# A two-layer trunk on one core: TensorE's order in the RWKV stage pinned by rounds, and the chunk's triangular system solved in two halves of 64 tokens

## The chip, the core and the metric

The kernel runs on one core of one Trainium2 chip. The time is device microseconds from start to end of one execution; lower is better. Beside the timed runs there is one profiled execution, whose trace gives the start and length of every instruction on every engine. TensorE (PE in the trace) does matmuls and transposes, each with a weight load (PEld); VectorE is DVE, ScalarE is ACT, GpSimd is POOL, and SyncE (SP) issues the loads.

## The reference, cut to what matters

One sequence of 256 tokens with 2048 channels passes an RWKV-7 layer and then an attention layer, each followed by a squared-ReLU MLP. The change touches only the RWKV-7 mixer, whose core is a recurrence over tokens for 32 heads of 64 channels:

```python
rkv = jnp.einsum('jbtd,jde->jbte', xs[:3], w_rkv)
...
def step(S, inp):
    r_t, w_t, k_t, v_t, kk_t, a_t = inp
    sa = jnp.einsum('bhvk,bhk->bhv', S, -kk_t)
    S = (S * w_t[:, :, None, :]
         + sa[..., None] * (kk_t * a_t)[:, :, None, :]
         + v_t[..., None] * k_t[:, :, None, :])
    y_t = jnp.einsum('bhvk,bhk->bhv', S, r_t)
    return S, y_t
```

The kernel does it in two chunks of 128 tokens. Within a chunk the step becomes a unit lower triangular system of 128 unknowns for each head; its inverse, transposed, is what the kernel calls `Tt`. The chunks are joined by the state `S`.

## The kernel before

Weights come in as float32 and are used as a sum of two reduced-precision parts: `hilo` makes `whi` on ACT (L162) and `wlo` on DVE (L163), and a product is three matmuls (`mm3w`, L213 to L215: hi times hi, hi times lo, lo times hi). A weight unit of 128x2048 is cast in two halves of 1024 columns. Each half also calls `pump`, which deals out the later layers' conditioning vectors: one step is a load and a DVE multiply with a sum over 128x1024 (L310).

The RWKV stage has 16 tiles of 128 channels (two heads each). For tile i two things are made:

- `project_rk(i)`, the products for r and k: 2 weights by 16 channel blocks by 3 matmuls of 256 columns, all into the PSUM bank `rk`. It gives way after every second channel block, 16 times in all.
- `rwkv_tile(i)`, the recurrence, a generator of 27 pieces with a `yield` between them. In order: 1 loads of small weights; 2 decay and gate (`wa`, the scan `cum`); 3 to 5 norms and scaled r, k (`st`, `AR`, `bt`, `kt`); 6 the masked matrices `MB` (`pm<-AR,bt`, then ACT copies and a POOL mask); 7 transposes (`tr`, `bk`); 8 the 16x16 diagonal blocks `Dg` spread out into `Z` on DVE; 9 the matmul `ar<-Z` (L710) and the matrices `MK` (`pm<-AR,kt`); 10 to 12 fifteen steps of forward substitution on DVE, two small instructions each (`xt<-ar,X` L722 and `X<-X,xt` L723), then ACT copies into `T16` and a DVE transpose `Tn` (L748); 13, 14 join blocks of 16 to 32 (`pW` L753, `pN` L762); 15, 16 join 32 to 64 (L777, L785); 17 to 19 join 64 to 128 (transpose `pT` L793, `pW` L799, `pN` L805, with ACT copies into `T64`, `W64` and `Tt`); then for chunk 0 `U = Tt * rhs` (`pu` L825), the state (`psS`) and the output (`py`), for chunk 1 the right side (`prhs<-S`), `pu` and `py`; then a group norm (`mean`, `var`, an inverse root of ten tiny DVE instructions) and the gated output (`yt`).

The driver (L903 on) works in rounds. A tile is started every STAGGER = 9 rounds, up to three fly at once, and in each round every flying tile does one piece, oldest first. So three tiles stand nine pieces apart: piece 9 of one shares its round with piece 18 of the tile before and piece 27 of the one before that. After the pieces, `16 / STAGGER` parts of the next tile's r and k products are recorded.

Recording isn't issuing. A scheduler takes the recorded program, plays its own timing model, and writes a fixed queue for each engine; when two instructions are ready it prefers the one recorded earlier. On the chip each engine then works through its queue strictly in that order. PSUM tiles go round in pools (`rt` and `rb` with 2 banks each, `mm` 2, `rk` 1), and `whi`/`wlo` have 2 buffers each.

When the last tile has started, `out_start` (the output projection's first 12 blocks, `pos`) takes the place of the r and k products.

Of the kernel before, what the change touches and what calls it, by code (L numbers as in the profile page):

```python
# [20 lines left out]
P = 128  # L21
D = 2048
KT = D // P
T = 256
# [9 lines left out]
STAGGER = 9  # L34
XV = 2
RATE_R = 0.85
RATE_T = 0.75
PACE = 2.5
RATE_M = 0.68
RATE_L = 0.25  # L40
RATE_H = 1.0
# [35 lines left out]
def trunk_kernel(ctx: ExitStack, tc: tile.TileContext, a, out, dbg=None):  # L77
# [300 lines left out]
    with ExitStack() as s0:  # L378
# [162 lines left out]
        with ExitStack() as s2:  # L541
# [9 lines left out]
            def tmp(tag, shape=(T,), bufs=1, dt=F32):  # L551
                return p5.tile([P, *shape], dt, tag=tag, name=tag, bufs=bufs)
# [13 lines left out]
            def project_rk(i):  # L566

                ps = banks["rk"].tile([P, 512], F32, tag="rk", name="rk")
                res = []
                for w, name in enumerate(("wr", "wk")):  # L570
                    raw = load(a[name][i])
                    o = slice(w * T, (w + 1) * T)
                    for half in range(2):
                        hi = split["hi"].tile([P, 1024], F32R, tag="whi", name="whi")
                        lo = split["lo"].tile([P, 1024], F32R, tag="wlo", name="wlo")
                        hilo(hi, lo, raw[:, half * 1024 : half * 1024 + 1024])
                        pump(rate[0])
                        for j in range(8):
                            kt = half * 8 + j
                            s = slice(j * P, (j + 1) * P)  # L580
                            mm3w(ps[:, o], hi[:, s], lo[:, s], xs_at(w, 0, kt), xs_at(w, 1, kt), kt == 0, kt == KT - 1)
                            if j % 2:
                                yield
                    res.append(tmp("rk"[w] + "S"))
                    ACT.copy(res[w], ps[:, o])  # L585
                rks[i] = res

            def rwkv_tile(i):
                K1 = DL + 1

                def tbank(name, k):
                    return banks[k].tile([P, 512], F32, tag=k, name=name)
# [80 lines left out]
                def At(m):  # L673
                    return MB[:, m // 2, m % 2, 0, :]
# [113 lines left out]
                yield  # L788

                lo, hi = slice(0, 64), slice(64, 128)  # L790
                pT = tbank("pT", "rt")
                for m_ in range(4):
                    PE.transpose(pT[lo, m_ * 64 : m_ * 64 + 64], Tt[lo, m_, lo], ident[lo, lo])  # L793
                T64 = tmp("T64", (4, 64))
                ACT.copy(T64[lo], pT[lo, :T].rearrange("p (m t) -> p m t", m=4))
                yield
                pW = tbank("pW", "rt")
                for m_ in range(4):
                    PE.matmul(pW[hi, m_ * 64 : m_ * 64 + 64], At(m_)[lo, hi], T64[lo, m_, :], start=True, stop=True)  # L799
                W64 = T64  # L800
                ACT.copy(W64[hi], pW[hi, :T].rearrange("p (m t) -> p m t", m=4))
                yield
                pN = tbank("pN", "rt")
                for m_ in range(4):
                    PE.matmul(pN[lo, m_ * 64 : m_ * 64 + 64], W64[hi, m_, :], Tt[hi, m_, hi], start=True, stop=True)  # L805
                ACT.copy(Tt[lo, :, hi], pN[lo, :T].rearrange("p (m t) -> p m t", m=4))
                yield

                S = tmp("S", (P,), 2)
                POOL.memset(S, 0.0)  # L810
                py = banks["py"].tile([P, 512], F32, tag="py", name="py")
                for c in range(2):
                    if c:
                        pr = tbank("prhs", "rb")
                        PE.matmul(pr[:, :P], AR[:, c, 0, :], S, start=True, stop=False)
                        for h in range(2):
                            vs = V[:, c, i * P + h * 64 : i * P + h * 64 + 64]
                            PE.matmul(pr[:, h * 64 : h * 64 + 64], MK[:, h, c, 0, :], vs, start=False, stop=(h == 1))
                        rh = tmp("rh", (P,), 3)
                        ACT.copy(rh, pr[:, :P])  # L820
                        yield
                    pu = tbank("pu", "rb")
                    for h in range(2):
                        q = slice(h * 64, h * 64 + 64)
                        PE.matmul(pu[:, q], Tt[:, 2 * h + c, :], rh[:, q], start=True, stop=True)  # L825
                    U = tmp("U", (P,), 2)
                    ACT.copy(U, pu[:, :P])
                    yield
                    if c == 0:
                        psS = tbank("psS", "rb")  # L830
                        for h in range(2):
                            q = slice(h * 64, h * 64 + 64)
                            vs = V[:, 0, i * P + h * 64 : i * P + h * 64 + 64]
                            PE.matmul(psS[q, :64], bk[:, q], U[:, q], start=True, stop=False)
                            PE.matmul(psS[q, :64], bk[:, P + h * 64 : P + h * 64 + 64], vs, start=False, stop=True)
                            ACT.activation(S[q, q], psS[q, :64], AF.Copy, scale=sc[q, 1:2])
                    else:
                        PE.matmul(py[:, P:T], AR[:, c, 1, :], S, start=True, stop=False)
                    for h in range(2):
                        q = slice(h * 64, h * 64 + 64)  # L840
                        vs = V[:, c, i * P + h * 64 : i * P + h * 64 + 64]
                        o = py[:, c * P + h * 64 : c * P + h * 64 + 64]
                        PE.matmul(o, MB[:, h, c, 1, :], U[:, q], start=(c == 0), stop=False)
                        PE.matmul(o, MK[:, h, c, 1, :], vs, start=False, stop=(c == 0 or h == 1))
                    if c == 0:
                        yield
# [2 lines left out]
                mean = tmp("mean", (4,))  # L849
                DVE.tensor_reduce(mean, py3, AX.X, ALU.add)  # L850
                DVE.tensor_scalar(mean, mean, 1.0 / 64, None, ALU.mult)
                yield
                tr = tbank("tr", "rb")
                for c in range(2):
                    PE.transpose(tr[:, c * P : (c + 1) * P], V[:, c, i * P : (i + 1) * P], ident)
# [45 lines left out]
            for _ in project_rk(0):  # L901
                pass
            flying, nxt, steps = [], 0, 0  # L903
            fill, owed, pace = iter(()), 0.0, 16 / STAGGER
            while nxt < KT or flying:
                if nxt < KT and len(flying) < LONG and steps >= STAGGER * nxt:
                    for _ in fill:
                        pass
                    flying.append(rwkv_tile(nxt))
                    nxt += 1  # L910
                    if nxt < KT:
# [1 line left out]
                    else:  # L913
# [3 lines left out]
                            "p (t k) c -> p t (k c)", t=2)  # L917
                        fill, pace = out_start(), PACE
                        rate[0] = RATE_T
                steps += 1  # L920
                for g_ in list(flying):
                    if next(g_, 0) == 0:
                        flying.remove(g_)

                owed += pace if flying else 48
                while owed >= 1:
                    owed -= 1
                    next(fill, 0)
            for _ in fill:
                pass  # L930
            for i in range(KO, KT):
# [632 lines left out]
```

## Time and profile before

| | |
|---|---|
| Timed runs | 2624.5, 2628.51, 2627.69 us; median 2627.69 |
| Profiled execution | 2610.6 us, span of its instructions 2608.9 us, granted TensorE clock 0.989 |
| Busy over the span | PE 96%, PEld 80%, DVE 75%, ACT 50%, POOL 3% |
| HBM read | 589.89 MB, 227 GB/s over the span |
| RWKV stage | first `rk` product at 211.7 us, last `pos` at 795.7 us |
| In 441.00 to 472.00 us (31 us) | PE busy 29.25, DVE 25.34, ACT 19.22, POOL 3.20 us |

PE's matmuls are pipelined, so their lengths overlap: an `rk` matmul lasts 0.28 us in the trace, but the next one starts 0.12 us later. What counts for a queue is therefore the step from start to start. "Idle before" in brackets is time the engine stood still, with what ended it. The granted clock is given for a stretch; 1.00 is full speed.

### The profile page before, as it was taken

The numbers are of one execution on the slowest core, as the hardware profiler recorded it, in microseconds if no ns is written. First come the engines' busy times: TensorE is split into PE (matmuls) and PEld (weight loads), VectorE is DVE, ScalarE is ACT, GpSimd is POOL, SyncE is SP. The second block draws the span as 40 slices with busy tenths as digits, with TensorE's granted clock in tenths as the row PEclk, the third lists the DMA queues.
The fourth block names the chain that finished last, engine by engine and source line by source line (L and its number), as shares of the span: only waits on it lengthen the run. The fifth ranks groups of instructions, "written<-read, shape, count | busy, mean of one in ns | idle before, by whom it ended". The sixth has DMA issues, their size and how long they took to land.

```text
span 2608.9 us, 39245 instructions
## 1 busy us (share of the span) xinstructions
PE 2510.7 (96%) x15048; PEld 2077.0 (80%) x15048; DVE 1950.6 (75%) x3823; ACT 1314.7 (50%) x2361; POOL 65.9 (3%) x150
## 2 busy tenths in 40 slices
PE   6998999999997999999999999999899999999998
PEld 3667888888776888888888878788788888888886
DVE  4797888888877788888888868777677655565555
ACT  4555666666745444444444446544544444444443
POOL 0000111011100000000000000000000000000000
PEclk9999999999999999999999999999999999999999
DMA  9755444444466588888888834657657555555553
GB/s 374 304 192 202 155 170 157 166 158 171 167 227 258 201 337 316 329 332 325 333 316 331 328 140 139 211 178 263 219 210 260 192 193 187 187 191 194 187 186 127
DMA packets 87885, 594.54 MB, mean 228 GB/s; under 512 B 10128, under 2 KB 14480, under 8 KB 16784
## 3 DMA queue, kind: packets, MB, share of 16 engines
q1 hardware_dynamic: 87696, 592.03, 62.9%
q8 instruction: 118, 1.93, 0.3%
q14 instruction: 71, 0.58, 0.1%
HBM read 589.89 MB, written 2.10 MB: 227 GB/s over the span
## 4 chain that ended last, share of the span: by engine, by line
PE 87%; DVE 7%; ACT 3%; DMA 2%; issue 1%; POOL 0%; SPq 0%; DVEq 0%; ACTq 0%
PE pup L223 17%; PE pd L208 9%; PE pd L210 9%; PE pd L209 9%; PE pup L224 9%; PE rk L213 2%; PE rk L215 2%; PE rk L214 2%; PE pm L658 2%; DVE wlo L163 2%; PE po L209 1%; PE po L210 1%; PE po L208 1%; PE pv L209 1%; PE pv L210 1%
## 5 line engine op out<-in xcount | busy, mean ns | idle before, releaser
L162 ACT CAST whi<-raw 128x1024 fp32r<-128x1024 f32 x729 | 743.7, 1023 | 882.7 <-PE pd L210 356.3
L163 DVE TENSOR_TENSOR wlo<-raw,whi 128x1024 fp32r<-128x1024 f32 x729 | 865.2, 1189 | 430.1 <-ACT whi L162 427.0
L223 PE MATMUL pup<-h,whi 128*128 128x512 f32 x1920 | 677.8, 398 | 0.0
L224 PE MATMUL pup<-h,wlo 128*128 128x256 f32 x1920 | 539.7, 281 | 0.0
L223 PEld LDWEIGHTS pup<-h,whi 128*128 128x128 f32 x1920 | 361.0, 188 | 88.2
L208 PE MATMUL pd<-whi,uh 128*128 128x512 f32 x1024 | 399.2, 390 | 0.0
L210 PE MATMUL pd<-whi,ul 128*128 128x512 f32 x1024 | 398.9, 390 | 0.0
L209 PE MATMUL pd<-wlo,uh 128*128 128x512 f32 x1024 | 398.8, 389 | 0.0
L310 DVE SCALAR_TENSOR_TENSOR raw<-raw,crow 128x1024 f32<-128x1024 f32 x320 | 388.5, 1221 | 10.5 <-DMA raw<-in_adat_dram 10.2
L224 PEld LDWEIGHTS pup<-h,wlo 128*128 128x128 f32 x1920 | 363.4, 189 | 0.5
L210 PEld LDWEIGHTS pd<-whi,ul 128*128 128x128 f32 x1024 | 192.3, 188 | 40.2
L208 PEld LDWEIGHTS pd<-whi,uh 128*128 128x128 f32 x1024 | 192.3, 188 | 39.9
L209 PEld LDWEIGHTS pd<-wlo,uh 128*128 128x128 f32 x1024 | 192.3, 188 | 39.5
L213 PE MATMUL rk<-xs,whi 128*128 128x256 f32 x512 | 155.2, 303 | 2.8 <-ACT rS L585 2.2
L215 PE MATMUL rk<-xs,wlo 128*128 128x256 f32 x512 | 149.6, 292 | 2.0 <-DVE wlo L163 2.0
L214 PE MATMUL rk<-xs,whi 128*128 128x256 f32 x512 | 147.1, 287 | 0.0
L213 PEld LDWEIGHTS rk<-xs,whi 128*128 128x128 f32 x512 | 98.5, 192 | 13.8 <-issue 8.9
L215 PEld LDWEIGHTS rk<-xs,wlo 128*128 128x128 f32 x512 | 98.4, 192 | 4.7 <-DVE wlo L163 2.8
L214 PEld LDWEIGHTS rk<-xs,whi 128*128 128x128 f32 x512 | 98.5, 192 | 0.9
L722 DVE TENSOR_TENSOR xt<-ar,X 128x60 f32<-128x60 f32 (+14 forms) x240 | 49.5, 206 | 17.5 <-ACT ar L711 14.8
L1180 DVE TENSOR_TENSOR ya<-pd,ya 128x512 f32<-128x512 f32 x96 | 61.5, 682 | 0.0
L209 PE MATMUL pv<-wlo,xsv 128*128 128x512 f32 x128 | 52.8, 413 | 5.5 <-DVE wlo L163 5.3
(431 smaller groups left out, 3671.3 us busy)
## 6 DMA issues: line engine op xcount, KB each, us to landing
raw<-in_adat_dram SPq DMA_DIRECT2D x160, 1024.0 KB, 6.9
raw<-in_up_dram SPq DMA_DIRECT2D x128, 1024.0 KB, 4.9
raw<-in_dn_dram SPq DMA_DIRECT2D x128, 1024.0 KB, 4.9
early<-in_ada_dram SPq DMA_DIRECT2D x17, 1024.0 KB, 11.6
raw<-in_wr_dram SPq DMA_DIRECT2D x16, 1024.0 KB, 4.9
raw<-in_wk_dram SPq DMA_DIRECT2D x16, 1024.0 KB, 5.0
raw<-in_wo_dram SPq DMA_DIRECT2D x16, 1024.0 KB, 5.8
raw<-in_mo_dram SPq DMA_DIRECT2D x16, 1024.0 KB, 4.9
```

The source lines that it names most:

```text
L162: ACT.copy(hi, x)
L163: return DVE.tensor_sub(lo, x, hi.bitcast(F32))
L208: PE.matmul(ps, lh, rh, start=start, stop=False)
L209: PE.matmul(ps, lh, rl, start=False, stop=False)
L210: PE.matmul(ps, ll, rh, start=False, stop=stop)
L213: PE.matmul(ps, wh, xh, start=start, stop=False)
L214: PE.matmul(ps, wh, xl, start=False, stop=False)
L215: PE.matmul(ps, wl, xh, start=False, stop=stop)
L223: PE.matmul(ps, hi[:, s], x2[:, kt].rearrange("p e t -> p (e t)"), start=(kt == 0), stop=False)
L224: PE.matmul(ps[:, T:], lo[:, s], x2[:, kt, 0, :], start=False, stop=(kt == KT - 1))
L310: DVE.scalar_tensor_tensor(raw[:, s], raw[:, s], 1.0, crow[:, s], ALU.mult, ALU.mult, accum_out=part[:, kt, half : half + 1])
L1180: DVE.tensor_add(y, pss[t], y)
```

## The change

1. Each round's recording is put into a block in which TensorE's order is kept as recorded (`tc.manual_schedule`), until `out_start` begins. As the built queues show, the order is kept within the block of one round; the first rows of a block can still move ahead of the rest of an earlier block.
2. `project_rk` gives way after every channel block (32 parts), and `LEAN` says how many parts each of the nine rounds gets, in place of an even share.
3. Pieces 17 to 19 are gone. `Tt` stays block diagonal (two blocks of 64). Each chunk is solved by halves instead: `U[lo] = Tt[lo] * rhs[lo]` (`pu`), then `rhs[hi] += A * U[lo]` (`pA` on PE, an addition of 64x128 on DVE, new line L817), then `U[hi] = Tt[hi] * rhs[hi]` (`pu`). That is four more yields, three fewer for the pieces gone, and one taken out after `mean`: a tile still has 27 pieces.
4. In `psS` the two products with `U` stand before the two with `V`, and the scaling copies after both.

```diff
--- before.py
+++ after.py
@@ -36,6 +36,8 @@
 RATE_R = 0.85
 RATE_T = 0.75
 PACE = 2.5
+
+LEAN = (7, 1, 5, 3, 5, 3, 1, 7, 0)
 RATE_M = 0.68
 RATE_L = 0.25
 RATE_H = 1.0
@@ -579,8 +581,7 @@
                             kt = half * 8 + j
                             s = slice(j * P, (j + 1) * P)
                             mm3w(ps[:, o], hi[:, s], lo[:, s], xs_at(w, 0, kt), xs_at(w, 1, kt), kt == 0, kt == KT - 1)
-                            if j % 2:
-                                yield
+                            yield
                     res.append(tmp("rk"[w] + "S"))
                     ACT.copy(res[w], ps[:, o])
                 rks[i] = res
@@ -788,24 +789,6 @@
                 yield
 
                 lo, hi = slice(0, 64), slice(64, 128)
-                pT = tbank("pT", "rt")
-                for m_ in range(4):
-                    PE.transpose(pT[lo, m_ * 64 : m_ * 64 + 64], Tt[lo, m_, lo], ident[lo, lo])
-                T64 = tmp("T64", (4, 64))
-                ACT.copy(T64[lo], pT[lo, :T].rearrange("p (m t) -> p m t", m=4))
-                yield
-                pW = tbank("pW", "rt")
-                for m_ in range(4):
-                    PE.matmul(pW[hi, m_ * 64 : m_ * 64 + 64], At(m_)[lo, hi], T64[lo, m_, :], start=True, stop=True)
-                W64 = T64
-                ACT.copy(W64[hi], pW[hi, :T].rearrange("p (m t) -> p m t", m=4))
-                yield
-                pN = tbank("pN", "rt")
-                for m_ in range(4):
-                    PE.matmul(pN[lo, m_ * 64 : m_ * 64 + 64], W64[hi, m_, :], Tt[hi, m_, hi], start=True, stop=True)
-                ACT.copy(Tt[lo, :, hi], pN[lo, :T].rearrange("p (m t) -> p m t", m=4))
-                yield
-
                 S = tmp("S", (P,), 2)
                 POOL.memset(S, 0.0)
                 py = banks["py"].tile([P, 512], F32, tag="py", name="py")
@@ -819,20 +802,35 @@
                         rh = tmp("rh", (P,), 3)
                         ACT.copy(rh, pr[:, :P])
                         yield
-                    pu = tbank("pu", "rb")
+
+                    pu = tbank("pu", "rt")
                     for h in range(2):
                         q = slice(h * 64, h * 64 + 64)
-                        PE.matmul(pu[:, q], Tt[:, 2 * h + c, :], rh[:, q], start=True, stop=True)
+                        PE.matmul(pu[lo, q], Tt[lo, 2 * h + c, lo], rh[lo, q], start=True, stop=True)
                     U = tmp("U", (P,), 2)
-                    ACT.copy(U, pu[:, :P])
+                    ACT.copy(U[lo], pu[lo, :P])
+                    yield
+                    pu = tbank("pA", "rt")
+                    for h in range(2):
+                        q = slice(h * 64, h * 64 + 64)
+                        PE.matmul(pu[hi, q], At(2 * h + c)[lo, hi], U[lo, q], start=True, stop=True)
+                    DVE.tensor_add(rh[hi], pu[hi, :P], rh[hi])
+                    yield
+                    pu = tbank("pu", "rt")
+                    for h in range(2):
+                        q = slice(h * 64, h * 64 + 64)
+                        PE.matmul(pu[hi, q], Tt[hi, 2 * h + c, hi], rh[hi, q], start=True, stop=True)
+                    ACT.copy(U[hi], pu[hi, :P])
                     yield
                     if c == 0:
                         psS = tbank("psS", "rb")
-                        for h in range(2):
-                            q = slice(h * 64, h * 64 + 64)
+                        halves = [slice(h * 64, h * 64 + 64) for h in range(2)]
+                        for q in halves:
+                            PE.matmul(psS[q, :64], bk[:, q], U[:, q], start=True, stop=False)
+                        for h, q in enumerate(halves):
                             vs = V[:, 0, i * P + h * 64 : i * P + h * 64 + 64]
-                            PE.matmul(psS[q, :64], bk[:, q], U[:, q], start=True, stop=False)
                             PE.matmul(psS[q, :64], bk[:, P + h * 64 : P + h * 64 + 64], vs, start=False, stop=True)
+                        for q in halves:
                             ACT.activation(S[q, q], psS[q, :64], AF.Copy, scale=sc[q, 1:2])
                     else:
                         PE.matmul(py[:, P:T], AR[:, c, 1, :], S, start=True, stop=False)
@@ -849,7 +847,6 @@
                 mean = tmp("mean", (4,))
                 DVE.tensor_reduce(mean, py3, AX.X, ALU.add)
                 DVE.tensor_scalar(mean, mean, 1.0 / 64, None, ALU.mult)
-                yield
                 tr = tbank("tr", "rb")
                 for c in range(2):
                     PE.transpose(tr[:, c * P : (c + 1) * P], V[:, c, i * P : (i + 1) * P], ident)
@@ -901,11 +898,12 @@
             for _ in project_rk(0):
                 pass
             flying, nxt, steps = [], 0, 0
-            fill, owed, pace = iter(()), 0.0, 16 / STAGGER
+            fill, owed, pace = iter(()), 0.0, 0
             while nxt < KT or flying:
                 if nxt < KT and len(flying) < LONG and steps >= STAGGER * nxt:
-                    for _ in fill:
-                        pass
+                    with nullcontext() if pace else tc.manual_schedule(engines={mybir.EngineType.PE}):
+                        for _ in fill:
+                            pass
                     flying.append(rwkv_tile(nxt))
                     nxt += 1
                     if nxt < KT:
@@ -917,15 +915,16 @@
                             "p (t k) c -> p t (k c)", t=2)
                         fill, pace = out_start(), PACE
                         rate[0] = RATE_T
+                with nullcontext() if pace else tc.manual_schedule(engines={mybir.EngineType.PE}):
+                    for g_ in list(flying):
+                        if next(g_, 0) == 0:
+                            flying.remove(g_)
+
+                    owed += (pace or LEAN[steps % STAGGER]) if flying else 48
+                    while owed >= 1:
+                        owed -= 1
+                        next(fill, 0)
                 steps += 1
-                for g_ in list(flying):
-                    if next(g_, 0) == 0:
-                        flying.remove(g_)
-
-                owed += pace if flying else 48
-                while owed >= 1:
-                    owed -= 1
-                    next(fill, 0)
             for _ in fill:
                 pass
             for i in range(KO, KT):

```

What the scheduler made of it, at three places of a tile in the middle of the stage. Lines in the new kernel stand one to three numbers off the old ones before the solve. First PE's queue around `pW<-Tn`, the first instruction that needs the end of the forward substitution. Before:

```order
L855 MATMUL tr<-ident,V 128x128 x2
L679 MATMUL tr<-ident,bt 128x128
L680 MATMUL tr<-ident,kt 128x128
L753 MATMUL pW<-Tn,A_5368 32x16 x16
L213 MATMUL rk<-xs,whi 128x256
L214 MATMUL rk<-xs,whi 128x256
L215 MATMUL rk<-xs,wlo 128x256
```

And now:

```order
L809 MATMUL pu<-rh,Tt_1987 64x64 x2
L754 MATMUL pW<-Tn,A_5584 32x16 x16
L633 MATMUL st<-kc,bt 128x2 x2
L215 MATMUL rk<-xs,whi 128x256
L216 MATMUL rk<-xs,whi 128x256
L217 MATMUL rk<-xs,wlo 128x256
```

Before, the next tile's norms, matrices `MB` and transposes (pieces 4, 6 and 7) stood ahead of this `pW`; now it stands in the round in which it was recorded, ahead of the next tile's piece 4 (`st`). Between the `ar` of the same tile and this `pW` stood 72 `rk` rows before, and 39 now; between `pW` and the next tile's `ar` stood 24, and now 57.

DVE's queue at the end of the same forward substitution (`wlo` is a half weight's low part, `raw<-raw,crow` a conditioning step). Before:

```order
L650 TENSOR_TENSOR kt<-kt,pinv 128x256
L722 TENSOR_TENSOR xt<-ar,X 128x4
L163 TENSOR_TENSOR wlo<-raw,whi 128x1024
L723 TENSOR_TENSOR X<-X,xt 128x4
L850 TENSOR_REDUCE mean<-py 128x4
L310 SCALAR_TENSOR_TENSOR raw,adpart<-raw,crow 128x1024
L748 STREAM_TRANSPOSE Tn<-T_5577 128x128
```

And now:

```order
L312 SCALAR_TENSOR_TENSOR raw,adpart<-raw,crow 128x1024
L622 TENSOR_TENSOR sc<-sc,cum 128x1
L724 TENSOR_TENSOR X<-X,xt 128x4x2
L638 SCALAR_TENSOR_TENSOR AR<-th,cum 128x2x128
L723 TENSOR_TENSOR xt<-ar,X 128x4
L639 TENSOR_TENSOR AR<-rS,cum 128x2x128
L724 TENSOR_TENSOR X<-X,xt 128x4
L650 SCALAR_TENSOR_TENSOR rb<-rS,pcol,kt 128x256
L165 TENSOR_TENSOR wlo<-raw,whi 128x1024
L749 STREAM_TRANSPOSE Tn<-T_5805 128x128
L651 TENSOR_TENSOR kt<-kt,pinv 128x256
L635 TENSOR_SCALAR rinv<-st 128x4
```

The substitution still has its 30 small instructions with `wlo`, `raw` and `AR` rows among them. What the queue holds between the last `Z` and `Tn` is 50 to 56 instructions now (54 to 78 before), three `wlo` of 1024 columns among them and two to four conditioning steps; and the DVE rows that answer to PE rows behind `pW` (`rinv<-st`) now stand behind `Tn`.

PE's queue from `ar` on. Before:

```order
L799 MATMUL pW<-T_4915,MB 64x64 x4
L710 MATMUL ar<-Z,kc 128x384 x2
L805 MATMUL pN<-Tt_1991,T_4915 64x64 x4
L825 MATMUL pu<-rh,Tt_1991 128x64 x2
L213 MATMUL pg<-sgh,whi 128x256
L214 MATMUL pg<-sgl,whi 128x256
```

And now:

```order
L816 MATMUL pA<-U,MB 64x64 x2
L711 MATMUL ar<-Z,kc 128x384 x2
L659 MATMUL pm<-AR,kt 128x256 x4
L822 MATMUL pu<-rh,Tt_1987 64x64 x2
L829 MATMUL psS<-U,bk 64x64 x2
L832 MATMUL psS<-V,bk 64x64 x2
L841 MATMUL py<-U,MB 128x64
L842 MATMUL py<-V,MK 128x64
```

The join of 64 to 128 (L799, L805) has gone from beside `ar`; `psS`, which needs the ACT copy of the `pu` ahead of it, now follows that `pu` at once, where twelve `pg` and `wa` rows stood between.

## The prediction

> **What bounds the stage now.** The page's slices show PE busy nearly everywhere, which says nothing about one stage. So I read the RWKV stage by itself: first the chain of work that ended last, to see how long a tile takes and which instructions pace it.
>
> ```profile
> 265.44 0.88 PE pW L753 x32
> ...
> 463.59 1.49 PE ar L710 x4
> ...
> 479.93 0.63 PE pm L658 x4
> 482.31 0.63 PE pm L658 x4
> 484.99 0.81 PE pW L753 x32
> 486.47 0.82 PE pN L762 x32
> ...
> 493.25 1.49 PE ar L710 x4
> ...
> 673.11 0.81 PE pW L753 x32
> ```
>
> First and last of 14 `pW<-Tn` are 407.7 us apart: 13 periods of 31.4 us, one per tile. Inside a period there are two parts: from `ar` to this tile's `pW` 21.4 us, and from `pW` to the next `ar` 8.3 us. The `pm` at 479.93 and 482.31 belong to the next tile's piece 6: before, that tile runs on while this one's substitution is unfinished.
>
> Then the busy time of each engine in these two parts and over the stage (columns: PE, PEld, DVE, ACT, POOL, granted clock, DMA share, GB/s):
>
> ```profile
> 463.50:484.90 21.40, 20.80 (x162) 18.04 (x160) 18.34 (x61) 14.35 (x36) 2.17 (x5) 1.00 0.40 127
> 484.90:493.20 8.30, 8.30 (x136) 6.93 (x135) 6.42 (x26) 5.76 (x22) 0.79 (x2) 1.00 0.44 157
> 224.00:689.00 465.00, 445.78 (x4328) 379.47 (x4328) 385.88 (x1266) 308.17 (x831) 55.48 (x102) 0.99 0.49 167
> ```
>
> PE is busy 96% of the stage and DVE 83%. Two engines are close to the limit, and what the order must do is keep both fed.
>
> For PE's prices I take steps, from the timeline of PE:
>
> ```profile
> 466.55 0.68 PE L805 MATMUL pN<-Tt,T 64*64 64x64 f32 x8
> 467.83 0.66 PE L825 MATMUL pu<-rh,Tt 128*128 128x64 f32 x4 [0.60 <-ACT Tt L806]
> ...
> 477.17 0.56 PE L632 MATMUL st<-kc,bt 128*128 128x2 f32 x4
> 477.58 0.36 PE L213 MATMUL rk<-xs,whi 128*128 128x256 f32 x1
> 477.79 0.28 PE L214 MATMUL rk<-xs,whi 128*128 128x256 f32 x1
> ...
> 478.98 0.28 PE L215 MATMUL rk<-xs,wlo 128*128 128x256 f32 x1
> 479.10 0.55 PE L825 MATMUL pu<-rh,Tt 128*128 128x64 f32 x4
> 479.49 0.44 PE L838 MATMUL py<-S,AR 128*128 128x128 f32 x2
> ...
> 488.25 0.43 PE L777 MATMUL pW<-T,MB 32*32 32x32 f32 x8
> 488.61 0.39 PE L215 MATMUL rk<-xs,wlo 128*128 128x256 f32 x1
> ```
>
> From 477.79 to 478.98 are ten steps: an `rk` row costs 0.12 us (`pg` and `wa` the same). Four small full-height records cost 0.39 to 0.41 (`st`, `pu`), so 0.10 each. Eight records of 32x32 cost 0.36, thirty-two 0.81 (chain); four `pm` 0.63; eight of 64x64 some 0.62, so four cost 0.31. Each change between tile shapes adds about 0.1 (`rk` after `st`: 0.21 to the next). And at 466.55 the join of 64 to 128 ends in a wait: `pu` stands 0.60 us idle for ACT's `Tt`.
>
> DVE's prices come from its timeline over the substitution:
>
> ```profile
> 465.62 0.22 DVE L722 TENSOR_TENSOR xt<-ar,X 128x60 f32<-128x60 f32 x1 [0.64 <-ACT ar L711]
> ...
> 468.06 0.22 DVE L723 TENSOR_TENSOR X<-X,xt 128x56 f32<-128x56 f32 x1
> 468.31 0.21 DVE L722 TENSOR_TENSOR xt<-ar,X 128x52 f32<-128x52 f32 x1
> ...
> 470.30 1.23 DVE L163 TENSOR_TENSOR wlo<-raw,whi 128x1024 fp32r<-128x1024 f32 x1
> 471.44 0.19 DVE L722 TENSOR_TENSOR xt<-ar,X 128x36 f32<-128x36 f32 x1
> ...
> 475.69 0.18 DVE L722 TENSOR_TENSOR xt<-ar,X 128x20 f32<-128x20 f32 x1
> 475.78 0.42 DVE L647 TENSOR_TENSOR kt<-kS,kt 128x256 f32<-128x256 f32 x1
> 476.11 0.17 DVE L723 TENSOR_TENSOR X<-X,xt 128x20 f32<-128x20 f32 x1
> 476.20 1.22 DVE L310 SCALAR_TENSOR_TENSOR raw<-raw,crow 128x1024 f32<-128x1024 f32 x1
> 477.34 0.17 DVE L722 TENSOR_TENSOR xt<-ar,X 128x16 f32<-128x16 f32 x1
> ...
> 482.05 0.16 DVE L723 TENSOR_TENSOR X<-X,xt 128x4 f32<-128x4 f32 x1
> ...
> 484.31 0.31 DVE L748 STREAM_TRANSPOSE Tn<-T 128x128 f32<-128x128 f32 x1 [0.40 <-ACT T L744]
> ...
> 489.63 0.29 DVE L704 TENSOR_TENSOR Z<-Dg,kc 128x128 f32<-128x128 f32 x1
> ```
>
> An `xt` or `X` that needs the one just before it costs 0.25 us, one with a stranger ahead of it about 0.1; a `wlo` or a conditioning step 1.14; 256 elements 0.33. From the first `xt` to `Tn` pass 18.7 us, of which the 30 small instructions are only some 5: the rest is `wlo`, conditioning and the next tile's vectors, in DVE's queue between them. From `Tn` to `pW` is 0.6 us.
>
> **The change, part by part.**
>
> *The solve by halves.* Gone are four `pT`, eight `pW` L799, eight `pN` L805 and eight `pu`: about 0.3 + 0.6 + 0.6 + 0.8, with 0.4 of shape changes and the 0.60 wait, 3.3 us of PE a tile. New are six groups of four 64-row records at 0.31 plus 0.1 to 0.2 of shape change, 2.5 us. A gain of 0.8 us if PE sets the pace. ACT loses three copies and two of `U`, gains four half ones; it is busy 308 of 465 us and not late. DVE gains two additions of 64x128, no row of which exists: bounds are 0.1 (a small step) and 0.33 (256 elements); I take 0.2, so 0.4 us.
>
> *`psS` behind its own `pu`.* A new wait of the kind of the 0.60 above, with `py`, `pg` and `wa` behind it. It lies in the part in which PE will have time (next), so it costs nothing here; without that cover 0.6 us a tile, 8 in all. The reordering inside `psS`, the yield after `mean`, POOL's memset of `S` and the one pair of loads that swaps on SP's queue: nothing, since their engines wait for none of it (POOL 55 of 465 us), at most some 0.1 us a tile.
>
> *The order and the deal.* This decides. PE can't pass `pW` before `Tn`. Between `ar` and `pW` PE now has: `ar` 1.5, eight `pm` 1.3, 39 `rk` and 12 `pg`/`wa` at 0.12, 6.1, two 64-row groups 0.8, 28 small records (`psS`, `py`, `prhs`) 2.8, the `psS` wait 0.6, shape changes 0.6: 13.7 us. DVE needs, between the last `Z` and `Tn`, by its new queue: 15 `X` rows in direct succession 3.75, 15 others 1.5, three `wlo` 3.4, two to four conditioning steps (mean 3.6) 4.1, eleven rows of 256 elements 3.6, small ones 0.4, ACT's `T16` and `Tn` 1.2: 18.0 us. With 0.6 to `pW` and some 0.4 by which the last `Z` ends after `ar` starts, 19.0 us. So PE stands still about 5.3 us at `pW`, every tile. Behind it wait `st`, nine `rk`, `pA` and `pN`; and DVE itself then waits for `st`, `pA` and `pN`, so neither engine uses the time.
>
> From `pW` to the next `ar` PE has 57 `rk` 6.8, `pW` and `pN` 1.6, four groups of eight 1.45, eight `pm` 1.3, four 64-row groups 1.6, 20 small records 2.0, shape changes 0.5: 15.2 us, where 8.3 stood before. DVE has some 11 us in that time and waits for PE. The other chain there is `pm` to ACT's `MB`, POOL's mask, `A32`, `Dg`, `Z`, `ar`. In the trace the last `pm` ends at 482.94 and the last `Z` at 489.92, 7.0 us, and the first `ar` needs only the first half of `Z`, some 0.5 earlier; PE has 6.4 us of work between `pm` and `ar` now (33 of the `rk` rows, `tr`, `pN`, two 64-row groups, `yt`), so I add 0.2.
>
> Period: 19.0 + 15.2 + 0.2 = 34.4 us against 31.4, +3.0. The same prices on the old queue give 20.8 and 8.0 where the trace has 21.4 and 8.3, so they run a little low. It holds for the 13 periods from tile 1's `ar` to tile 14's, +39; the first one has less on DVE, about +2; in the last, unpinned tiles and `out_start`, 0.8 us twice is gained: +39 us.
>
> *The clock.* After a still PE the granted clock falls. These are two neighbouring stretches early in the stage, and PE rows in the second:
>
> ```profile
> 235.10:238.50 3.40, 1.24 (x8) 0.81 (x10) 3.40 (x9) 1.92 (x6) 0.10 (x1) 1.00 0.31 108
> 238.50:241.90 3.40, 3.40 (x17) 2.75 (x14) 1.65 (x4) 1.67 (x5) 1.27 (x2) 0.50 0.32 58
> ...
> 239.78 0.42 PE L214 MATMUL rk<-xs,whi 128*128 128x256 f32 x1
> 239.99 0.42 PE L215 MATMUL rk<-xs,wlo 128*128 128x256 f32 x1
> ```
>
> PE was busy 1.24 of 3.4 us, and for the next 3.4 us the clock was 0.50 and an `rk` step 0.21 us. Such a stretch loses up to 3.4 x (1 - 0.12/0.21) = 1.5 us. A stop of 5.3 us at `pW` should bring one each tile, partly spent in the stop itself: bounds 0 and 3 (two stretches), I take 1.2, near one stretch, as in the row. Thirteen times: +16.
>
> [...]
>
> Sum: +39 + 16 = +55 us. On the profiled execution 2610.6 + 55 = 2666; the median of the runs shown stands 17.1 above that execution, so I forecast 2627.7 + 55 = 2683 us.
>
> **Rivals.** *PE alone sets the pace: faster.* If the forward substitution ended within PE's 13.7 us, a tile would take PE's work, 13.7 + 15.2 = 28.9 plus the wait at `ar` 0.2: -2.3 us, 13 times, -30, and the loss of the clock gone too: 2598. It decides from a substitution of 12.7 us on. For it: the 30 small instructions alone are 5 to 7 us, and PE's share is the higher one. Against it: 12 us of other rows stand between them in a queue that is fixed. Chance 0.10.
>
> *Half of it: the waits of before make room.* DVE is idle 17% of the stage, some 5 us a period, for instance
>
> ```profile
> DVE xt L722 <- ACT ar L711: 13.6, 10, 2.8
> DVE T L764 <- PE pN L762: 8.9, 10, 2.5
> ```
>
> (us in total, times, longest). If idle time fell from 5 to under 3.5, DVE's whole queue would set the period. By the same prices it has, between `Tn` and the last `Z`, one `wlo`, two conditioning steps, twelve rows of 256 elements and some twenty small ones at 0.2, 11.5 us; with the 18.0 that is 29.5, and the period 31.4 to 33.3: no change to +25. For it: the first wait shrinks, since three rows stand ahead of `xt` now. Against it: the second grows, as `pN` now comes after `pW` and nine `rk`. Chance 0.05 for within 0.2%, and 0.12 for +6 to +25.
>
> *The clock takes more.* If each stop brings two slow stretches, by the rows above they cost 2.9 us instead of 1.2, and the forecast becomes 39 + 38 = +77, 2705; with `psS` uncovered +85, 2713. For it: a stop of 5.3 us reaches into two stretches of 3.4. Against it: the second follows on 15 us of dense work. Chance 0.15. The forecast itself, +25 to +70: 0.58.
>
> **How the numbers follow.** Faster by over 0.2% (5 us, about what a measurement here can tell from no change) 0.10; within it 0.05; slower 0.85. The range leaves out the faster and equal cases, the near end of the half case and the far end of the clock, 0.2 in all: +10 to +84 us, 2638 to 2712.
>
> **What would show it.** In the new trace: `pW<-Tn` periods of 34 to 36 us; PE idle 4 to 6 us before L754, ended by DVE `Tn`; the largest wait of the stage there, and DVE's wait for `pN` or `pA` grown; clock 0.50 stretches between 245 and 700 us, about one a tile. Wrong would be: no wait at L754; `X` rows that end within 13 us of `ar`; periods below 31. Then my count of DVE's queue, or the cost of its rows, is at fault.

## The result, and the profile after

| | before | after |
|---|---|---|
| Timed runs, median (range) | 2626.9 us (2624.5 to 2628.51) | 2764.85 us (2759.36 to 2771.44) |
| Ratio to before | | 1.0529, interval 1.0493 to 1.0565 |
| Span of the profiled execution | 2608.9 us | 2760.7 us |
| Granted TensorE clock over the span | 0.989 | 0.945 |

The kernel is 138 us slower; +55 were forecast, and +84 at most. The direction and the stop at `pW` came as forecast. The loss by the clock did not.

First the page of the kernel after: the granted clock in 40 slices of the span, and the group of the 32x32 products at which the stop was expected (busy us, mean ns of one, idle us just before them and what ended most of it).

```profile
PEclk8998788788879999999999999999999999999999
L754 PE MATMUL pW<-Tn,A 32*32 32x16 f32 x512 | 19.5, 205 | 68.5 <-DVE Tn L749 68.5
```

In before every slice of `PEclk` reads 9. Now nine slices of the RWKV stage (the fourth to the twelfth) read 7 or 8, and one line of PE has idled for 68.5 us. The waits of PE in after, over the pinned part of the stage (us in total, times, longest):

```profile
PE pW L754 <- DVE Tn L749: 62.9, 13, 6.4
PE psS L829 <- ACT U L823: 13.9, 13, 1.1
PE pN L786 <- ACT Tt L788: 7.6, 13, 0.8
```

That is 4.8 us at `pW` for each tile on average: the stop of the forecast (5.3). The wait at `psS` is 1.1 and not 0.6 us, but it lies in the part in which PE waits for DVE anyway. The waits of DVE over the same time:

```profile
DVE mean L848 <- PE py L842: 41.6, 12, 4.9
DVE rinv L635 <- PE st L633: 28.8, 13, 2.4
DVE rh L817 <- PE pA L816: 21.3, 13, 1.8
```

That is 92 us, where before had 7 in its stage, with no `pA`:

```profile
DVE rinv L634 <- PE st L632: 3.8, 8, 0.8
DVE mean L850 <- PE py L844: 3.3, 5, 1.0
```

What stands behind `pW` on PE (`st`, `pA`, and later `py`) keeps DVE waiting. PE and DVE take turns. The chain of work that ended last gives the tiles' rhythm:

```profile
275.90 1.33 PE pW L754 x32
295.98 1.49 PE ar L711 x4
314.98 1.29 PE pW L754 x32
...
476.47 1.30 PE pW L754 x32
503.45 1.49 PE ar L711 x4
523.25 1.29 PE pW L754 x32
...
803.30 1.29 PE pW L754 x32
```

In the two tiles shown, 19.0 and 19.8 us pass from `ar` to `pW` (forecast 19.0; over 13 tiles 17.5 to 20.6, mean 19.1), and 20.1 and 27.0 us from `pW` to the next `ar`, where 15.4 were forecast (mean 22.0). The 13 periods from 275.90 to 803.30 are 40.6 us long, against 31.4 before and 34.4 in the forecast. So the missing time is in the part in which PE works, and the windows of the tile at 476 us show why. Columns: stretch, its length, busy time (instructions) of PE, PEld, DVE, ACT, POOL, granted clock, DMA share, GB/s.

```profile
467.80:471.21 3.41, 3.41 (x31) 3.28 (x29) 3.41 (x13) 2.81 (x7) 0.00 (x0) 1.00 0.11 38
471.21:474.63 3.42, 0.14 (x3) 0.00 (x0) 3.42 (x12) 0.26 (x1) 0.10 (x1) 1.00 0.01 2
474.63:478.04 3.41, 1.57 (x34) 1.57 (x34) 0.93 (x7) 1.07 (x4) 0.00 (x0) 0.50 0.65 197
478.04:481.45 3.41, 3.41 (x18) 3.07 (x18) 0.95 (x4) 0.87 (x2) 0.00 (x0) 0.50 0.29 118
481.45:484.87 3.42, 3.42 (x44) 3.24 (x44) 2.40 (x5) 1.96 (x7) 0.15 (x1) 0.50 0.00 0
484.87:488.28 3.41, 3.41 (x23) 3.12 (x21) 1.81 (x4) 0.28 (x2) 0.00 (x0) 0.50 0.36 67
488.28:491.70 3.42, 3.42 (x21) 2.52 (x20) 1.02 (x3) 0.26 (x1) 0.00 (x0) 0.50 0.67 278
491.70:495.11 3.41, 3.38 (x21) 2.81 (x19) 1.11 (x5) 2.66 (x7) 1.27 (x2) 0.50 0.00 0
495.11:498.52 3.41, 3.10 (x20) 2.69 (x21) 1.72 (x9) 2.51 (x10) 0.00 (x0) 0.50 0.77 264
498.52:501.94 3.42, 3.42 (x18) 3.42 (x18) 1.70 (x6) 0.02 (x1) 0.00 (x0) 0.50 0.13 48
501.94:505.35 3.41, 3.41 (x20) 2.17 (x21) 2.50 (x5) 1.53 (x4) 0.00 (x0) 1.00 0.36 62
```

The stop fills the second stretch (PE busy 0.14 us), and then the clock is 0.50 for eight stretches, 27.3 us, though PE is busy for 3.10 us or more in seven of them. It comes back only after 498.52 to 501.94, in which PE runs nothing but `rk`. PE's timeline shows the step there, 0.21 us, and 0.12 once the clock is back:

```profile
501.43 0.41 PE L216 MATMUL rk<-xs,whi 128*128 128x256 f32 x1
501.65 0.41 PE L217 MATMUL rk<-xs,wlo 128*128 128x256 f32 x1
501.86 0.33 PE L215 MATMUL rk<-xs,whi 128*128 128x256 f32 x1
502.03 0.28 PE L216 MATMUL rk<-xs,whi 128*128 128x256 f32 x1
502.15 0.28 PE L217 MATMUL rk<-xs,wlo 128*128 128x256 f32 x1
```

Over the stage there are 236 us at half clock, in 21 stretches of 3.4 to 27.3 us, and each of the 14 stops at `pW` is followed by one of 6.8 us or more; before had 7 us in two. This sum, taken from the clock records between the first `rk` and the last `pos`, is called "half-clock time" below. It is that of one profiled execution each, so differences of a few tens of us are not read from it.

### The profile page after: what moved, and what is told of

The parts are those of the page before. It is cut to its first block, busy times and chain, and to the rows that moved or that the text cites. A ratio compares the mean times of both kernels' runs of the same rounds, so it can differ in the third digit from the quotient of the medians.

```text
span 2760.7 us, 39143 instructions
## 1 busy us (share of the span) xinstructions
PE 2581.0 (93%) x14984; PEld 2145.5 (78%) x14984; DVE 1981.0 (72%) x3855; ACT 1309.6 (47%) x2345; POOL 56.7 (2%) x150
## 4 chain that ended last, share of the span: by engine, by line
PE 77%; DVE 10%; ACT 3%; issue 1%; DMA 0%; DVEq 0%; ACTq 0%
PE pup L225 16%; PE pd L210 8%; PE pd L212 8%; PE pd L211 8%; PE pup L226 8%; DVE wlo L165 2%; PE rk L215 2%; DVE raw L312 2%; PE rk L216 2%; PE rk L217 2%; DVE xt L723 1%; PE po L211 1%; DVE X L724 1%; PE po L212 1%; PE po L210 1%
## 5 line engine op out<-in xcount | busy, mean ns | idle before, releaser
L210 PEld LDWEIGHTS pd<-whi,uh 128*128 128x128 f32 x1024 | 192.2, 188 | 40.1
L215 PE MATMUL rk<-xs,whi 128*128 128x256 f32 x512 | 176.2, 344 | 3.4 <-ACT rS L586 1.3
L217 PE MATMUL rk<-xs,wlo 128*128 128x256 f32 x512 | 165.4, 323 | 1.9 <-DVE wlo L165 1.9
L216 PE MATMUL rk<-xs,whi 128*128 128x256 f32 x512 | 164.8, 322 | 0.0
L215 PEld LDWEIGHTS rk<-xs,whi 128*128 128x128 f32 x512 | 118.4, 231 | 15.6 <-issue 7.2
L217 PEld LDWEIGHTS rk<-xs,wlo 128*128 128x128 f32 x512 | 118.5, 231 | 3.2 <-DVE wlo L165 3.0
L216 PEld LDWEIGHTS rk<-xs,whi 128*128 128x128 f32 x512 | 119.4, 233 | 0.0
L754 PE MATMUL pW<-Tn,A 32*32 32x16 f32 x512 | 19.5, 205 | 68.5 <-DVE Tn L749 68.5
L754 PEld LDWEIGHTS pW<-Tn,A 32*32 32x32 f32 x512 | 18.2, 140 | 70.7 <-issue 63.5
```

What stands on the lines that cost most here:

```text
L210: PE.matmul(ps, lh, rh, start=start, stop=False)
L215: PE.matmul(ps, wh, xh, start=start, stop=False)
L216: PE.matmul(ps, wh, xl, start=False, stop=False)
L217: PE.matmul(ps, wl, xh, start=False, stop=stop)
```

## The experiments

A run's half-clock time and period (mean over the 13 tiles between the second `ar` and the fifteenth; after 41.1 us, before 31.4) come from its own trace. The kernel before, run beside them, took 2622 to 2628 us.

**The change in parts.** `e1_no_pin`: after, with both blocks opened as `nullcontext()`, so LEAN's deal and the halves with a free scheduler.

> The change with its deal of the r and k products and its solve by halves, but TensorE's order left to the scheduler in every round. Theory A (the kept order makes PE stop at pW<-Tn, and the stop costs the clock): the stop is gone, no pW wait over 1 us, half clock in the stage under 20 us in all, a period near 31 us, total 2605 to 2635 us. Rival B (the 64-row pieces of the solve, or the uneven deal, lower the clock by themselves): half clock stretches stay, total above 2680 us.

Measured: 2680.27 us, ratio 1.0224 [1.0174, 1.0275]; half-clock time 137 us; period 36.1. The stop is all but gone, its longest wait 1.4 us:

```profile
PE pW L754 <- DVE Tn L749: 4.4, 7, 1.4
```

But the half clock stays, as rival B has it, and the time is at the border of B's range. The pin adds 85 us to what the other two parts cost.

`e2_pin_only`: before, with the order kept in each round, the old deal (`pace = 16 / STAGGER`) and the old solve.

> The kernel before with the order kept within a round and nothing else: old solve with the join of 64 to 128, old even deal. In its queue 42 rk rows stand between ar and pW<-Tn and 54 behind. Theory A: stops of 4 to 6 us at pW, half clock in more than 150 us of the stage, 2710 to 2780 us. Rival B: no more than the stops, 14 x 3 us, clock as before: 2640 to 2680 us.

Measured: 2740.69 us, 1.0444 [1.0424, 1.0463]; half-clock time 181 us; period 40.1, as theory A has it. The stop is there without the halves and without LEAN (PE's waits):

```profile
PE pW L753 <- DVE Tn L748: 43.8, 11, 5.9
```

`e3_halves`: before, with the solve by halves, the regrouped `psS` and no yield after `mean`; nothing pinned.

> The kernel before with the solve by halves (and the reordered psS, and without the yield after mean), old deal, order left to the scheduler. Theory A: 0.8 us of PE less a tile, no stop, 2605 to 2630 us. Rival B: the 64-row pieces lower the clock: over 100 us of half clock, above 2680 us.

Measured: 2684.41 us, 1.0234 [1.0171, 1.0296]; half-clock time 99 us; period 34.8. The gain of theory A is out. The four runs stand at 2670.5, 2670.6, 2698.3 and 2702.7 us, and the trace is that of the fastest.

`e10_psmean`: before, with the two small edits of `e3_halves` alone, and `e9_deal`: before, with LEAN and 32 parts alone, nothing pinned.

```diff
-                            if j % 2:
-                                yield
+                            yield
...
-                owed += pace if flying else 48
+                owed += (pace or LEAN[steps % STAGGER]) if flying else 48
```

> The kernel before with the two small parts of the change alone: psS with its products regrouped, and no yield after mean; the solve as before. Theory A (the loss of e3_halves is the solve's: small tiles and its waits): 2615 to 2640, under 25 us at half clock. Theory B (most of the loss of e3_halves is the shifted grouping of pieces that the scheduler sees): 2650 to 2690, with 40 to 100 us at half clock and 10 us or more of rk waiting for its bank.

> The kernel before with the deal alone: a yield after every channel block and LEAN's counts, the scheduler free, the old solve. Theory A (a free scheduler spreads the rk products again, as e1_no_pin stood level with e3_halves): 2615 to 2645, under 30 us at half clock in the stage. Theory B (the bunched deal alone makes windows with a low share of the array): 30 to 100 us at half clock, 2645 to 2690.

Measured: `e10_psmean` 2622.4 us, 1.0003 [0.9983, 1.0023]; `e9_deal` 2633.81 us, 1.005 [1.0027, 1.0073], half-clock time 55 us. Both times are theory A's, both half-clock times B's. The small edits cost nothing, though that profiled execution has 44 us at half clock: this is how far such a sum says little. The deal alone costs 11 us, the halves alone 59, the pin alone 115, and all three 138. They don't add up, and `e1_no_pin` stands level with `e3_halves`: beside the halves the deal isn't shown to add anything.

What the halves lose was first put down to their small tiles. PE's timeline in `e3_halves` shows something plainer, 15 times with 16.6 us in all:

```profile
633.28 0.38 PE L851 MATMUL tr<-ident,V 128*128 128x128 f32 x2
634.73 0.39 PE L213 MATMUL rk<-xs,whi 128*128 128x256 f32 x1 [1.07 <-ACT rS L585]
```

and ACT's timeline in the same place:

```profile
633.36 1.04 ACT L162 CAST whi<-raw 128x1024 fp32r<-128x1024 f32 x1 [1.70 <-PE rk L214]
634.31 0.36 ACT L585 COPY rS<-rk 128x256 f32<-128x256 f32 x1
```

In this kernel's queue a weight cast of 1.04 us stands on ACT ahead of the copy that frees the bank `rk`, so PE waits 1.07 us at nearly every tile. In before the same line of PE waited 2.8 us in all. The other part follows 5 us later: in the row from 640.00 PE is busy 3.10 us, but with 77 instructions, 64 of them on 32x32 tiles, and the clock falls for four stretches, of which the first two are shown. How the 59 us divide between these two parts was not tested.

```profile
640.00:643.42 3.42, 3.10 (x77) 2.77 (x77) 1.31 (x7) 1.90 (x8) 0.68 (x2) 1.00 0.71 230
643.42:646.83 3.41, 3.41 (x22) 3.23 (x22) 0.94 (x4) 1.70 (x6) 0.00 (x0) 0.50 0.91 382
646.83:650.24 3.41, 3.41 (x25) 2.25 (x24) 1.56 (x6) 0.51 (x2) 0.00 (x0) 0.50 0.02 7
```

**How much of it is the clock.** `e4_warm`: after, with 40 products ahead of `pW` in 13 tiles, into the unused half of `py`'s bank, long enough to fill the stop.

```diff
+                    if c and i < KT - 3:
+                        for z in range(WARM):
+                            w = xs_at(0, 0, z % KT)
+                            PE.matmul(py[:, T:], w[:, :P], w, start=True, stop=True)
```

> The change with 40 additional products of 256 columns (4.8 us) just ahead of pW<-Tn in 13 tiles, written into an unused half of the py bank, so that PE is busy while it would have stood still. Their results are not used. Theory A: the clock stays at 1.00 but for a few stretches, the period is the one without the clock's loss, 34 to 35.5 us against 40.6, total 2655 to 2690 us although PE does 62 us more work. Rival B (small-tile rows, not the stop, hold the clock down): half clock stays over 150 us, total 2750 us or more.

Measured: 2696.82 us, 1.028 [1.0262, 1.0298]; half-clock time 38 us; period 36.2. Time and period lie a little above theory A's ranges; rival B, with 150 us and 2750, is out. 520 needless matmuls made the kernel 68 us faster than after.

`e5_cold`: the same 520, on a tile of 32x32.

```diff
-                            PE.matmul(py[:, T:], w[:, :P], w, start=True, stop=True)
+                            PE.matmul(py[:32, T:], w[:32, :32], w[:32], start=True, stop=True)
```

> The kernel after with the same 40 fill-in products of 256 columns ahead of pW as in the run before, but each on a tile of 32x32 in place of 128x128 (they add work, the outputs stay). Theory A (the clock goes by the share of the array that works in a window of 3.4 us: 32x32 is a sixteenth of it, so the fill-in counts as idleness): the half-clock time in the stage stays at 200 us or more, as in the kernel after (236), and the time is 2740 to 2800. Theory B (only idle time lowers the clock, any matmul keeps it up): as with the large fill-in, 30 to 60 us at half clock and 2690 to 2710.

Measured: 2794.24 us, 1.0651 [1.0616, 1.0686]; half-clock time 297 us; period 43.4. The two fill-ins on the pages, of `e4_warm` and then of `e5_cold`, with the clock by slices:

```profile
PEclk8999899999999999999999999999999999999999
L816 PE MATMUL py<-xs 128*128 128x256 f32 x520 | 65.8, 285 | 0.0
```

```profile
PEclk8999877877877999999999999999999999999999
L816 PE MATMUL py<-xs 32*32 32x256 f32 x520 | 69.3, 291 | 0.0
```

As many products, of 285 and 291 ns on average, leave 38 us at half clock in one and 297 in the other. In `e5_cold` the stop is gone as well (4.9 us of wait at `pW` in all), and still, in the windows around one fill-in (526.9 to 531.8 us), the clock halves after a stretch in which PE has no idle time and runs almost only the fill-in:

```profile
524.92:528.33 3.41, 3.41 (x31) 3.03 (x31) 3.29 (x12) 1.93 (x5) 0.10 (x1) 1.00 0.00 0
528.33:531.75 3.42, 3.42 (x31) 2.82 (x28) 2.66 (x9) 0.83 (x3) 0.00 (x0) 1.00 0.11 38
531.75:535.16 3.41, 3.41 (x42) 3.15 (x42) 0.42 (x3) 0.31 (x1) 0.20 (x1) 0.50 0.03 5
```

So in this run the clock fell without idle time of PE ahead of it.

**The shape of the fill-in.** The same fill-in in four more shapes: `e11_cols32` with `w[:, :32]` as weights, `e12_zerow` with a 128x128 tile of zeros as weights, `e13_rows32` with 32 rows (`w[:32, :P], w[:32]`), `e14_rows64` with 64.

> As e5_cold (after with 40 fill-in products ahead of pW; the outputs stay), the fill-in on 128 rows by 32 columns of the array. Theory A1 (the share counts rows times columns): a quarter share, below the bound, so 200 to 300 us at half clock and 2750 to 2800, as with 32x32. Theory A2 (it counts busy rows only): as with 128x128, 30 to 60 us and 2690 to 2710.

> As e4_warm (40 fill-in products on 128x128 ahead of pW; the outputs stay), with all weights of the fill-in zero. Theory A1 (the share counts cells in use, whatever they hold): 30 to 60 us at half clock, 2690 to 2710. Theory A3 (it counts products that are not zero, which would explain why the larger tiles of e6_big and e8_lean_big, half zeros, brought nothing): 200 to 300 us at half clock, 2750 to 2800.

> As e4_warm (40 fill-in products ahead of pW; the outputs stay), the fill-in on 32 rows by 128 columns of the array. Theory A2 (rows in use count): as with 32x32, 200 to 300 us at half clock, 2760 to 2810. Theory A4 (only tiles that are small on both sides count as idle): as with 128x128, 30 to 60 us, 2690 to 2710.

> As e13_rows32 with 64 rows by 128 columns. [...] Theory A2f (64 rows count as full): 30 to 60 us, 2690 to 2710, so the 64-row tiles of the solve don't pull the clock down.

| fill-in, rows x columns | us (ratio, interval) | half-clock time |
|---|---|---|
| 128x128 (`e4_warm`) | 2696.82 (1.0262 to 1.0298) | 38 |
| 128x128, zeros (`e12_zerow`) | 2692.82 (1.0249 to 1.0311) | 31 |
| 128x32 (`e11_cols32`) | 2696.88 (1.0259 to 1.0312) | 41 |
| 64x128 (`e14_rows64`) | 2733.33 (1.0389 to 1.0447) | 130 |
| 32x128 (`e13_rows32`) | 2797.43 (1.0587 to 1.0729) | 256 |
| 32x32 (`e5_cold`) | 2794.24 (1.0616 to 1.0686) | 297 |

Among these six fill-ins the columns in use and the values make no difference that shows (31 to 41 us with 128 rows); the rows in use do, and 64 rows, with 130 us, stand between 32 and 128. My theory that the share of the array counts, rows times columns, fell with `e11_cols32`.

**Attempts to repair it.** `e6_big`: `e3_halves` with both `pu` over all 128 rows and columns of `Tt` (`pu[:, q]`, `Tt[:, 2 * h + c, :]`, `rh[:, q]`), and `pA` with 128 columns.

> The kernel before with the solve by halves (as in e3_halves), but both pu products over all 128 rows and columns of Tt and pA over 64x128, with the same number of columns streamed. Theory A (share of the array): the windows full of small tiles come up, the half-clock time in the stage falls from 99 to 30-75 us and the time from 2684 to 2650-2675. Theory B (the loss in e3 is that of its waits, rk for its bank above all, and the clock follows these): 75 to 110 us at half clock, 2675 to 2700.

Measured: 2675.52 us, 1.0193 [1.016, 1.0227]; half-clock time 123 us. The time lies at the border of the two ranges, the half-clock time above both, and the interval overlaps with that of `e3_halves`: no help from the larger tiles is shown.

`e7_lean`: after, with the `rk` products moved to between `ar` and `pW`. `e8_lean_big`: that, with the tiles of `e6_big`.

```diff
-LEAN = (7, 1, 5, 3, 5, 3, 1, 7, 0)
+LEAN = (5, 5, 5, 2, 1, 1, 1, 2, 10)
```

> The kernel after with LEAN = (5, 5, 5, 2, 1, 1, 1, 2, 10): 73 rk products lie between ar and pW in place of 39, so the stop at pW is filled, and few are left beside pieces 13 to 27. Both theories: the wait at pW falls from 68 us to under 15, waits at pN, pA, pu and pW of the later pieces grow to 2-5 us a tile. Theory A (share of the array): the stretch from pW to ar, now nearly all small tiles, falls under the share that keeps the clock up, so 120 to 250 us stay at half clock; 2690 to 2750. Theory B (the stop itself lowers the clock): under 70 us at half clock, 2640 to 2680.

> As e7_lean, with pu and pA on the larger tiles of e6_big. Theory A: less half-clock time than e7_lean by a quarter or more, 15 to 40 us faster than it. Theory B: as e7_lean within 8 us.

Measured: `e7_lean` 2735.49 us, 1.0426 [1.0387, 1.0465], half-clock time 232 us; `e8_lean_big` 2763.36 us, 1.0527 [1.0492, 1.0562], 297 us. `e7_lean` came as theory A has it, but the waits of 2 to 5 us a tile at later pieces did not come (`pN`, `pA`, `pu` and the later `pW` together under 1 us a tile). The stop at `pW` is gone from the list of PE's waits, whose largest in the stage is now

```profile
PE yt L869 <- DVE tha L865: 20.0, 12, 4.0
```

but the half-clock time is that of after. A full queue ahead of `pW` leaves the other part, from `pW` to `ar`, to products of 32 and 64 rows. That larger tiles made this worse by 28 us is a miss that I can't explain: in the stage the two traces differ in 177 of PE's 4315 places in the queue and in 280 of DVE's 1293.

None of the variants beats before, and no run pointed to one that would.

## Why the prediction was wrong

*The stop at `pW`: right.* `ar` to `pW` took 17.5 to 20.6 us, mean 19.1 (19.0), idle 4.8 us (5.3), released by `Tn`, and DVE waiting in its turn for what stands behind. The rival in which PE alone sets the pace is out.

*The order and the deal: right in kind, a third too low.* `e4_warm` shows the period with little of the half clock left: 36.2 us, +4.8 against before. Only 7 of its 38 us of half clock lie between the second `ar` and the fifteenth, 0.5 us a tile; an `rk` step of 0.21 in place of 0.12 loses at most 43% of that, 0.2 us. The fill-in itself may add 0.3 us (`ar` to `pW` takes 19.4 us on average). So without any half clock the period would be 35.7 to 36.2, and the term 13 x (4.3 to 4.8) = 56 to 62 us, where 39 were forecast. Part of it is 16.7 us from `pW` to `ar` in `e4_warm`, where the prices gave 15.4. And the sum set prices against a mean: the tile from which the prices were taken had 21.4 + 8.3 = 29.7 us and 28.8 by the prices, but the mean of before is 31.4. Prices against prices, the term is 34.4 - 28.8 = +5.6 a tile and not +3.0, above the 4.3 to 4.8 that came.

*The clock: the step that failed.* It was forecast at 1.2 us a tile (bounds 0 and 3), 16 in all. By the same two traces it is 41.1 - 36.2 to 41.1 - 35.7, so 4.9 to 5.4 us a tile, 64 to 70 us. The time beside it checks this: 201 us at half clock in these tiles, 15.5 each, of which at most 43% is lost, 6.6 us. I took "one stop, one stretch" from the row at 235.10 and 238.50, but there PE ran dense `rk` through most of its single slow stretch, and the pinned kernel has no such run of dense work right behind its stop. One slow stretch a stop did come, but of 6.8 to 27.3 us. Against the rival of two stretches of 3.4 us I argued that "the second follows on 15 us of dense work". That work is not dense. It is `rk` in groups of 3 to 21 between products of 32 and 64 rows, and in the tile shown above the clock returned only after a stretch of nothing but `rk`. Over the 20 returns of after between the first and the last `rk`, each follows a stretch in which PE had no idle time, with busy time times rows / 128 at 0.85 or more of the stretch in all but one (0.76); it stayed down behind stretches of up to 0.93. Even the rival's 2.9 us a tile is little more than half of what came.

The kernel before already held the warning, in the other of its two slow stretches. There PE had no idle time at all, but for most of the stretch ran products of 32 and 64 rows (`pW`, `pN`, `pm`), and then the clock halved:

```profile
293.10:296.50 3.40, 3.40 (x73) 2.67 (x71) 2.89 (x7) 1.76 (x5) 0.74 (x2) 1.00 0.36 72
296.50:299.90 3.40, 3.40 (x23) 3.11 (x22) 1.40 (x7) 2.22 (x9) 0.64 (x1) 0.50 0.70 280
```

And the 2.2 us idle in the row at 235.10 are parts of two gaps, of 1.02 and 1.55 us: no single long stop was needed there either.

Nor does PE's busy time alone tell the stretches apart. In the tile shown above, seven with PE busy for 1.57 to 3.42 us were each followed by another at half clock, and in `e5_cold` the one at 528.33, with 3.42 us, was followed by the first such stretch.

*The solve by halves: wrong in the free kernel, small in the pinned one.* I gave it a gain of 0.8 us of PE a tile. Alone, it costs 59 us: the 1.07 us stop at the bank `rk`, 16.6 us in all, which no price of an instruction can show since the scheduler's queue made it, and half clock, in shares that were not tested. Beside the pin, the halves and LEAN together add 24 us (2740.69 to 2764.85); how that divides was not tried. The addition of 64x128 took 0.29 us in DVE's timeline of after, inside the bounds 0.1 and 0.33.

*`psS` and the yield after `mean`: right.* Level with before in `e10_psmean`, and the wait of 1.1 us at `psS` is followed by the longer one at `pW`. The swapped loads were not tried alone.

In sum: forecast +39 and +16 within the 13 periods. Measured +126 there, 56 to 62 of it by the order and 64 to 70 by the clock; the rest of the 152 us between the two profiled spans lies before the second tile and after the fifteenth, and was not taken apart. These are figures of one profiled execution each: that of before was 16 us faster than its median, that of after 2 us, so by the medians the loss is 138 us.

## What to carry to other kernels

Before a queue is pinned on one engine, find the other engine's chain that the pin has to wait for, and count what is left to do there; a free scheduler had let the next tile's work pass `pW`. Read in the trace for how long a stop on TensorE leaves the clock down, and don't count its own length alone: here stops of 4.8 us on average were followed by 6.8 to 27.3 us at half clock, and the 20 returns counted in after each came behind a stretch of 3.4 us without idle time, in the tile shown one of nothing but full-height matmuls. Look whether the order has such stretches; here groups of 3 to 21 dense products stood between small-row ones. Look at stretches full of small-row products too: in before the clock halved behind one with PE busy for all of its 3.40 us (at 293.10). Where the stop can't go, a fill-in of needless 128-row products can pay, as it did here for half of the loss (2764.85 to 2696.82 us).

## What the runs showed of the hardware that I had not expected

- The half-clock time went with the rows that the fill-in used: the same number of products, 281 to 296 ns each, left 31 to 41 us with 128 rows, 130 with 64, and 256 to 297 with 32; 32 or 128 columns, and zeros or data, were alike. `e8_lean_big` doesn't fit: its `pu` had 128 rows in place of the 64 of `e7_lean`, and its half-clock time was longer (297 against 232 us).
- PE's busy time just before the clock fell and just before it came back differed. In after, between the first and the last `rk`, each of the 20 falls follows a stretch of 3.41 us with PE busy for at most 69% of it, and each of the 20 returns one without idle time; behind 31 more stretches without idle time the clock stayed at half. The falls are not like this in all runs: one of the two of before, and 51 of 192 in the 16 traces, follow a stretch in which PE had no idle time.
